# Attention outputs with channels on partitions, in a one-core layer of latent attention and gated linear attention

## The chip, the core and the metric

The kernel runs on one core of a Trainium2 chip. The metric is the device time of one execution in microseconds. Before the change it was 1341.73 us, the median of three runs (1340.36, 1341.73, 1341.91).

## The reference

One step of an encoder layer over 1024 prompt tokens and 64 tokens of a running stream, which has 512 cached frames. All is in float32. Cut to what the change touches:

```
mod = silu(c) @ w_ada + b_ada                      # six vectors per stream: shift, scale, gate, twice
h = rms_norm(x, g_norm1) * (1 + scale1) + shift1
c_q, c_kv, k_rope_raw, gq, gk, gv, g_lr, g_r = split(h @ w_in)

q = (rms_norm(c_q, g_q_lora) @ w_uq)               # 4 heads of 128 + 64
latent = concat([past_latent, rms_norm(c_kv, g_kv_lora)])
kv = latent @ w_ukv                                # per head 128 of key, 128 of value
k = concat([k_nope, krope])                        # the 64 rotary columns are the same for all heads
q, k = rms_norm(q, g_q_head), rms_norm(k, g_k_head)
q, k = rope on the last 64 columns
a_out = softmax(q k^T * scale, chunk-causal) @ v

b_out = rms_norm(gated linear attention) * silu(g_r)
x = x + gate1 * (concat([a_out, b_out]) @ w_out)
h2 = rms_norm(x, g_norm2) * (1 + scale2) + shift2
x = x + gate2 * (relu(h2 @ w_up)**2 @ w_down)
```

## The kernel before

Every large product is three products of a high and a low half (`mm3`, L92: high x high, low x high, high x low, in the type fp32r), so operands are split in two after they are made (`split`, L101, `split_T`, L954): ACT casts the high half, DVE subtracts it for the low half. Products of probabilities and values and all transposes are in plain float32. In the trace a plain product appears as two records on TensorE (PE), a transpose or an fp32r product as one.

The work of a stage is written as several generators, streams, that `interleave` (L47) advances by estimated times; the Tile framework's scheduler then puts the instructions of each engine in an order of its own, and each engine's queue runs in that order. DMAs are instructions of the queue that issues them, SP's nearly always; one that waits for its data holds all that stand behind it in that queue. Buffers come from pools with a fixed number of places: a load into a place waits until the last reader of its old content is done.

The stages in order of time:

- *Start* (to about 90 us). `start` (L399) loads x and the weights' first columns, `scale_rows` and `scale_end` make the modulation's scale for the first and then the second half of the channels. ACT takes squares of x (L337), multiplies x by the gain (`gained_x`, L380, high half on ACT, low half on DVE) and, with DVE, splits the first weights (`split_first`, L325). `shifts` makes the shift vector with `mod_vec` and loads the last tokens of x (`load_x(2)`).
- *Projections and gated linear attention* (to about 260 us). Its outputs go through PE transposes to channels on partitions and to the DRAM tile `mix_d`, channel blocks 4 to 7; the output gate goes to `r_d`.
- *Keys of the cached frames* (to about 360 us), `past_keys` (L1144), beside the last projections. A tile of 128 cached latents is loaded as it lies in memory, tokens on partitions. Two PE transposes (L1154) bring it to channels on partitions, ACT and DVE split it (`lath`, `latl`), and `keys_values` (L961) makes keys and values of four heads. There, after the norm, PE transposes the 128 plain columns of four heads (L1002), and the 64 rotary columns of four heads (`krt`, L1009), each head's twice side by side in 128 columns, so that the transposed tile holds them on partitions 0 to 63 and again on 64 to 127. ACT casts all (L1010), DVE takes the high half from the lower partitions (L1011): the high halves stand on partitions 0 to 63 and the low halves on 64 to 127 of `kv.kr`.
- *Attention* (to about 560 us). `keys_stream` and `queries_stream` make keys and queries of the prompt's tiles, three `worker` streams take units of one tile of queries and one head: the tile of the 64 sample tokens first (tile 8), then tiles 0 to 7. `attend` (L1069) makes the scores (L1080), their maximum, and the exponentials with their sum (L1091); DVE takes the sum's reciprocal. PE transposes the probabilities in blocks of 128 keys (L1117, evicted to `pt`, L1120), and the product with the values (L1107) has `pt` as its stationary operand and the values as the moving one: queries on partitions. ACT evicts it scaled by the reciprocal of the sum (L1132), which is one number per partition there, into `mo`. When four heads of a tile are done, `worker` transposes `mo` by four PE transposes (L1221), ACT copies them to `mt` (L1223) and writes `mt` from its own queue to `mix_d`, blocks 0 to 3 (L1224). Beside it, `mods` makes three further modulation vectors with `mod_vec`: row blocks of `w_ada` of 512 KB are loaded into three places `raw` (L166) and used by PE in order (L178). `wo_early` splits five blocks of the output weights.
- *Output projection* (to about 690 us). `out_early` (L1273) fetches `mix_d` and the gates for the first quarter of the tokens while attention's last tiles run, multiplies blocks 4 to 7 by the gate (`gate`, L1270) and splits all. `main` (L1423) does the same for the other three quarters (`mx`, `mr`, L1428), one quarter ahead of PE, then the products, the residual and the sums of squares.
- *The MLP*, with products of the Strassen kind, to the end. The change does not touch it.

Of the kernel before, what the change touches and what calls it, by code (L numbers as in the profile page):

```python
# [72 lines left out]
def layer(ctx: ExitStack, tc: tile.TileContext, I, O):  # L73
# [80 lines left out]
    c_d = dram.tile([16, P], F32, name="c_d")  # L154

# [80 lines left out]
    def has(*keys):  # L236
        return lambda: all(k in done or k in groups for k in keys)
# [59 lines left out]
    with ExitStack() as sctx:  # L297
# [92 lines left out]
        def start():  # L390
# [101 lines left out]
        def shifts():  # L492
# [5 lines left out]
            load_x(2)  # L498
            SP.dma_start(wg[0:16], I["w_gate_up"])
            SP.dma_start(wg[96:97], I["b_gate_up"])  # L500
            SP.dma_start(indi, I["gla_ind"])
            done.add("x 2")
            yield from vec
# [105 lines left out]
    with gctx:  # L609
# [7 lines left out]
        def load_past(t, place):  # L617

            past[t] = place
            SP.dma_start(past[t], I["cache_mla_latent"][t * P:(t + 1) * P])  # L620

        load_past(0, dp.tile([P, 256], F32, name="past", bufs=1))
# [338 lines left out]
    def keys_values(lh, ll, ki, tab, n, kv, slot, ahead=4500):  # L961
# [4 lines left out]
        R = kw.tile([P, 1, 2, 64], F32, name="R")  # L966
# [5 lines left out]
        DVE.tensor_tensor(out=R[:n, 0, :, 0:32], in0=a[:n, :, 0:32].broadcast_to([n, 2, 32]),  # L972
                          in1=t_[:n, :, 32:64].broadcast_to([n, 2, 32]), op=ALU.subtract)
        DVE.tensor_tensor(out=R[:n, 0, :, 32:64], in0=a[:n, :, 32:64].broadcast_to([n, 2, 32]),
                          in1=t_[:n, :, 0:32].broadcast_to([n, 2, 32]), op=ALU.add)
        kr = kw.tile([P, H, P], F32, name="krt", bufs=1)
        for g in range(2):
# [6 lines left out]
            for j in range(2):  # L984
                ACT.activation(kr[:n, 2 * g + j], pg[:, j, 0:P], AF.Square, accum_out=ss[:n, 2 * g + j:2 * g + j + 1])
# [9 lines left out]
        for g in range(2):  # L995
            DVE.tensor_tensor(out=kr[:n, 2 * g:2 * g + 2], in0=R[:n].rearrange("p t d c -> p t (d c)").broadcast_to([n, 2, P]),
                              in1=rs[g], op=ALU.mult)
# [10 lines left out]
        for hd in range(H):  # L1008
            PE.transpose(tp[:, hd, :n], kr[:n, hd], ident[:n, :n])  # L1009
        ACT.copy(kv.kr[:, :, cs], tp[:, :, :n])  # L1010
        DVE.tensor_tensor(out=kv.kr[64:P, :, cs], in0=tp[64:P, :, :n], in1=f32(kv.kr[64:P, :, cs]), op=ALU.subtract)  # L1011
# [57 lines left out]
    def attend(i, hd, n, off, kvs, nkeys, masked):  # L1069
# [25 lines left out]
        DVE.reciprocal(st[:n, 6:7], st[:n, 4:5])  # L1095
# [6 lines left out]
        def pv(args):  # L1102
            pt, k0, kn_ = args
            for k in range(kn_):
                kt = k0 + k
                kw = min(P, nkeys - P * kt)
                PE.matmul(op[:n, 0:P], lhsT=pt[:kw, k, :n], rhs=kvs[kt // 4].v[:kw, kt % 4, hd],  # L1107
# [22 lines left out]
        if i not in mos:  # L1130
            mos[i] = aw.tile([P, H, P], F32, name="mo")
        ACT.activation(mos[i][:n, hd], op[:n, 0:P], AF.Copy, scale=st[:n, 6:7])  # L1132
# [11 lines left out]
    def past_keys():  # L1144
        kvS.append(KV(kvA, 512))
        kvN.append(KV(kvA, 64))
        for t in (1, 2):
            load_past(t, kw.tile([P, 256], F32, name="latr"))
        for t in range(4):
            lt = past[t]  # L1150
            yield 600, 0, has("UK")
            tp = tp_bank()
            for b in range(2):
                PE.transpose(tp[:, b * P:(b + 1) * P], lt[:, b * P:(b + 1) * P], ident)  # L1154
            lh = kw.tile([P, 2, P], F32R, name="lath")
            ll = kw.tile([P, 2, P], F32R, name="latl")
            if t == 0:
                load_past(3, dp.tile([P, 256], F32, name="past", bufs=1))
            v = tp[:, 0:256].rearrange("p (b t) -> p b t", b=2)
            ACT.copy(lh, v)  # L1160
# [875 lines left out]
```

## Time and profile before

| what | value |
|---|---|
| median of the runs shown | 1341.73 us |
| the profiled execution's own time | 1340.44 us |
| its span, first to last instruction | 1338.3 us |
| granted TensorE clock | 1.00 |
| DVE, ACT busy | 68%, 49% |
| DMA traffic | 189.15 MB, 141 GB/s in the mean |

A row of a group reads: line, engine, operation, output <- inputs, partitions x elements, xcount, then busy time in us and mean ns of one instruction, and idle time of its engine ahead of it with what ended it. For matmuls the form `128*64 128x128` gives rows and columns of the stationary operand, then partitions and columns of the moving one. PE's records overlap, so a group's busy time is not the time that it keeps others away; for that one looks at the starts in a timeline. In a timeline a row has start and duration in us. Rows of stretches give each engine's busy us with the number of instructions, then the granted clock, the share of DMA and GB/s.

### The profile page before, as it was taken

Reading aid. Unit: us, or ns where it says so; the run is one execution under the profiler, and the core shown is the slowest. Engines: PE = TensorE matmul, PEld = TensorE weight load, DVE = VectorE, ACT = ScalarE, POOL = GpSimd, SP = SyncE. Lnnn points to the kernel's source line nnn. Section 1 sums busy time; section 2 is a strip of 40 time slices with the busy share of each in tenths; the row PEclk is TensorE's granted clock in tenths of the full one; section 3 lists DMA queues with packets and bytes.
Section 4 is the critical chain, followed back from the end, with each engine's and each line's share of the span. In section 5 each row is a group of like instructions: output and inputs, shape, how many; then the busy total and the mean of one; then the engine's idle time right before and its main releaser. Section 6 shows DMA issues by size and latency. Waiting matters only on the chain.

```text
span 1338.3 us, 25907 instructions
## 1 busy us (share of the span) xinstructions
PE 1316.3 (98%) x9986; PEld 1252.8 (94%) x9986; DVE 910.9 (68%) x2050; ACT 652.6 (49%) x1625; POOL 75.4 (6%) x136
## 2 busy tenths in 40 slices
PE   9999999999999999999999999999999999999999
PEld 8899999888767898999999999999999999999998
DVE  4898787466576756676899877565545965864553
ACT  5375554454266657543674444444444333343332
POOL 0100010132122200000000000000000000000000
PEclk9999999999999999999999999999999999999999
DMA  9420122374445200752537554443259755543440
GB/s 342 145 75 1 48 77 88 108 225 124 134 139 173 67 17 25 225 176 90 169 111 230 172 194 150 138 156 123 110 196 347 253 167 187 158 130 88 134 127 34
DMA packets 157957, 189.15 MB, mean 141 GB/s; under 512 B 14654, under 2 KB 109194, under 8 KB 157706
## 3 DMA queue, kind: packets, MB, share of 16 engines
q1 hardware_dynamic: 150554, 181.98, 42.6%
q10 hardware_dynamic: 7280, 5.52, 1.3%
q8 instruction: 78, 1.28, 0.4%
q14 instruction: 45, 0.37, 0.1%
HBM read 134.00 MB, written 53.47 MB: 140 GB/s over the span
## 4 chain that ended last, share of the span: by engine, by line
PE 77%; DVE 10%; ACT 4%; DMA 4%; issue 2%; POOL 2%; ACTq 0%; SPq 0%; DVEq 0%; POOLq 0%
PE mm L94 14%; PE mm L96 13%; PE mm L95 13%; PE g L94 5%; PE g L96 5%; PE g L95 5%; PE tp L94 3%; PE tp L96 3%; PE tp L95 3%; PE mm L1080 3%; PE g L1107 2%; PE g L882 1%; PE tp L1117 1%; DVE ts L1822 1%; DMA wg<-in_w_gate 1%
## 5 line engine op out<-in xcount | busy, mean ns | idle before, releaser
L102 ACT CAST opers<-quad 128x512 fp32r<-128x512 f32 x112 | 69.3, 620 | 185.1 <-PE mm L96 147.6
L103 DVE TENSOR_TENSOR opers<-quad,opers 128x512 fp32r<-128x512 f32 x112 | 77.1, 689 | 114.7 <-ACT opers L102 114.7
L94 PE MATMUL mm<-opers 128*128 128x272 f32 x448 | 128.5, 287 | 0.3 <-DVE e L1964 0.3
L96 PE MATMUL mm<-opers 128*128 128x272 f32 x448 | 128.7, 288 | 0.0
L95 PE MATMUL mm<-opers 128*128 128x272 f32 x448 | 128.2, 286 | 0.0
L94 PE MATMUL mm<-ah,wh 128*128 128x272 f32 x424 | 121.8, 288 | 0.0
L96 PE MATMUL mm<-ah,wl 128*128 128x272 f32 x424 | 121.8, 288 | 0.0
L95 PE MATMUL mm<-al,wh 128*128 128x272 f32 x424 | 121.7, 287 | 0.0
L94 PE MATMUL mm<-hh,wh 128*128 128x384 f32 (+2 forms) x264 | 91.1, 346 | 0.7 <-ACT wh L329 0.7
L95 PE MATMUL mm<-hl,wh 128*128 128x384 f32 (+2 forms) x264 | 87.2, 330 | 0.0
L96 PE MATMUL mm<-hh,wl 128*128 128x384 f32 (+2 forms) x264 | 86.6, 329 | 0.0
L94 PEld LDWEIGHTS mm<-opers 128*128 128x128 f32 x448 | 84.5, 189 | 0.5 <-issue 0.5
L96 PEld LDWEIGHTS mm<-opers 128*128 128x128 f32 x448 | 84.2, 188 | 0.0
L95 PEld LDWEIGHTS mm<-opers 128*128 128x128 f32 x448 | 84.0, 188 | 0.0
L94 PEld LDWEIGHTS mm<-ah,wh 128*128 128x128 f32 x424 | 79.9, 188 | 0.0
L95 PEld LDWEIGHTS mm<-al,wh 128*128 128x128 f32 x424 | 79.8, 188 | 0.0
L96 PEld LDWEIGHTS mm<-ah,wl 128*128 128x128 f32 x424 | 79.6, 188 | 0.1
L103 DVE TENSOR_TENSOR opers<-ru,opers 128x544 fp32r<-128x544 f32 x108 | 77.6, 719 | 2.3 <-ACT opers L102 2.0
L102 ACT CAST opers<-ru 128x544 fp32r<-128x544 f32 x108 | 69.4, 643 | 13.2 <-PE mm L96 10.9
L102 ACT CAST wh<-ru 128x512 fp32r<-128x512 f32 x67 | 41.1, 619 | 66.6 <-PE tp L95 21.0
L94 PE MATMUL mm<-wh,hh 128*128 128x264 f32 (+3 forms) x216 | 65.7, 304 | 0.0
L96 PE MATMUL g<-opers 128*128 128x272 f32 x224 | 64.7, 289 | 0.0
(416 smaller groups left out, 4247.2 us busy)
## 6 DMA issues: line engine op xcount, KB each, us to landing
ru<-u_d SPq DMA_DIRECT2D x108, 272.0 KB, 2.8
raw<-in_w_ada SPq DMA_DIRECT2D x32, 512.0 KB, 4.4
ru<-in_w_up SPq DMA_DIRECT2D x32, 512.0 KB, 4.1
quad<-in_w_down SPq DMA_DIRECT2D x16, 1024.0 KB, 6.5
u_d<-st SPq DMA_DIRECT2D x60, 272.0 KB, 2.1
u_d<-sc SPq DMA_DIRECT2D x45, 272.0 KB, 2.2
raw<-in_w_in SPq DMA_DIRECT2D x22, 256.0 KB, 3.5
x<-in_xo_T SPq DMA_DIRECT2D x8, 544.0 KB, 5.7
```

Source lines behind the costliest of these rows:

```text
L94: pin(PE.matmul(out, lhsT=ah, rhs=bh, start=first, stop=False, skip_group_check=more))
L95: pin(PE.matmul(out, lhsT=ah, rhs=bl, start=False, stop=False, skip_group_check=more))
L96: pin(PE.matmul(out, lhsT=al, rhs=bh, start=False, stop=last, skip_group_check=more))
L102: ACT.copy(hi, src)
L103: eng.tensor_tensor(out=lo, in0=src, in1=f32(hi), op=ALU.subtract)
L882: PE.matmul(sc[:n, a, p], lhsT=d[:, w * p + n * a:w * p + n * a + n], rhs=qv[:, :, p, a], start=True, stop=True)
L1080: PE.matmul(sp[:n, :w], lhsT=x[:, hd, :n], rhs=y[:, hd, :w], start=(j == 0), stop=(j == 4))
L1107: PE.matmul(op[:n, 0:P], lhsT=pt[:kw, k, :n], rhs=kvs[kt // 4].v[:kw, kt % 4, hd], start=(kt == 0), stop=(kt == nkt - 1))
L1117: PE.transpose(tp[:kw, k, :n], pr[k0 // 4][:n, P * k:P * k + kw], ident[:n, :n])
L1822: DVE.scalar_tensor_tensor(out=ts[s][:, 0:256], in0=w[:, ks], scalar=1.0, in1=cb[:, s, ks], op0=ALU.mult, op1=ALU.mult, accum_out=sums[:, ...
```

## The change

Four edits.

1. *Attention's output.* In `attend` the two operands of the product with the values change places: the values are the stationary operand and `pt` the moving one, so the product has channels on partitions and queries along its columns. ACT copies it to `mo` without a scale. The reciprocals of the sums go to a small tile `rsum`, tokens on partitions. When four heads are done, `worker` writes `rsum` to a new DRAM tile `rs_d` with heads as rows, four bytes a piece, and `mo` to `mix_d`, both from SP's queue. The four transposes, the copy `mt` and its write from ACT's queue are gone. `out_early` and `main` load the rows of `rs_d` spread over all partitions (`b0`, `b3`, `mb`) and multiply blocks 0 to 3 by them on DVE.
2. *Rotary keys.* The rotary columns of a key are no longer doubled. Two heads stand side by side in the 128 columns of one transpose, so two transposes take the place of four. ACT's cast and DVE's subtraction become two each, over 64 partitions and two heads: for the even heads the high halves stand on the lower partitions, for the odd heads on the upper ones, as it comes.
3. *Cached latents.* The kernel's input is the cached latents transposed. They are loaded with channels on partitions and split as they are.
4. *Start.* The squares of x's second half are taken ahead of the wait for the modulation, and the weights' split ahead of the gained x. `load_x(2)` is written in two parts.

```
@@ attend
-        DVE.reciprocal(st[:n, 6:7], st[:n, 4:5])
+        if i not in mos:
+            mos[i] = aw.tile([P, H, P], F32, name="mo"), aw.tile([P, H], F32, name="rsum")
+        mo, rsum = mos[i]
+        DVE.reciprocal(rsum[:n, hd:hd + 1], st[:n, 4:5])
...
-                PE.matmul(op[:n, 0:P], lhsT=pt[:kw, k, :n], rhs=kvs[kt // 4].v[:kw, kt % 4, hd],
+                PE.matmul(op[:, :n], lhsT=kvs[kt // 4].v[:kw, kt % 4, hd], rhs=pt[:kw, k, :n],
                           start=(kt == 0), stop=(kt == nkt - 1))
...
-        ACT.activation(mos[i][:n, hd], op[:n, 0:P], AF.Copy, scale=st[:n, 6:7])
+        ACT.copy(mo[:, hd, :n], op[:, :n])
@@ worker
-                yield 0, 700, None
-                tp = heads(tp_bank())
-                for hd in range(H):
-                    PE.transpose(tp[:, hd, :n], mos[i][:n, hd], ident[:n, :n])
-                mt = aw.tile([P, H, P], F32, name="mt", bufs=1)
-                ACT.copy(mt[:, :, :n], tp[:, :, :n])
-                ACT.dma_start(mix_d[:, 0:4, off:off + n], mt[:, :, :n])
-                yield 450, 0, None
+                mo, rsum = mos.pop(i)
+                SP.dma_start(rs_d[:, off:off + n].rearrange("h t -> t h"), rsum[:n])
+                SP.dma_start(mix_d[:, 0:4, off:off + n], mo[:, :, :n])
+                yield 0, 0, None
@@ out_early, main
+    def sums_row(k, kn, t0, n):
+        return rs_d[k:k + kn, t0:t0 + n].rearrange("(o h) t -> o h t", o=1).broadcast_to([P, kn, n])
...
-        t0, t1, r1 = fetch(mix_d, 0, 3), fetch(mix_d, 4, 2), fetch(r_d, 0, 2)
+        t0, b0, t1 = fetch(mix_d, 0, 3), fetch(rs_d, 0, 3), fetch(mix_d, 4, 2)
+        fetch(rs_d, 3, 1, b3)
         yield 0, 3000, None
+        gate(t0, b0)
         halves(0, 3, t0)
+        r1, t3 = fetch(r_d, 0, 2), fetch(mix_d, 3, 1)
...
+                    SP.dma_start(mx[3][:, :, o:o + n], sums_row(0, H, t0, n))
...
+                    gate(mx[0], mx[3])
                     split(mh[:, 0:4], ml[:, 0:4], mx[0], DVE)
@@ keys_values
-        for hd in range(H):
-            PE.transpose(tp[:, hd, :n], kr[:n, hd], ident[:n, :n])
-        ACT.copy(kv.kr[:, :, cs], tp[:, :, :n])
-        DVE.tensor_tensor(out=kv.kr[64:P, :, cs], in0=tp[64:P, :, :n], in1=f32(kv.kr[64:P, :, cs]), op=ALU.subtract)
+        for g in range(2):
+            PE.transpose(tp[:, g, :n], kr[:n, g], ident[:n, :n])
+        for e in range(2):
+            hi, lo = slice(64 * e, 64 * e + 64), slice(64 - 64 * e, P - 64 * e)
+            ACT.copy(kv.kr[hi, e::2, cs], tp[hi, 0:2, :n])
+            DVE.tensor_tensor(out=kv.kr[lo, e::2, cs], in0=tp[hi, 0:2, :n], in1=f32(kv.kr[hi, e::2, cs]), op=ALU.subtract)
@@ past_keys
-            tp = tp_bank()
-            for b in range(2):
-                PE.transpose(tp[:, b * P:(b + 1) * P], lt[:, b * P:(b + 1) * P], ident)
...
+            lh, ll = split_T(kw, past[t], 2, P, "lat")
@@ start
+            squares(0, sq, (4,))
             yield 0, 0, has("mod 1 1")
-            squares(0, sq, (4,))
             for k in range(4, KT):
-                gained_x(k, 0, pin)
                 if k % 2 == 0:
                     split_first(1, 0, (k // 2,))
+                gained_x(k, 0, pin)
@@ shifts
-            load_x(2)
...
-            yield from vec
+            load_x(2, (0,))
+            for n, step in enumerate(vec):
+                yield step
+                if n == 4:
+                    load_x(2, (4,))
...
```

More of the change, by code (lines that the diff above doesn't have):

```diff
@@ L154, in layer @@
     c_d = dram.tile([16, P], F32, name="c_d")
+    rs_d = dram.tile([H, TOK], F32, name="rs_d")
     def mod_rows(m, k):
@@ L619, in load_past @@
             past[t] = place
-            SP.dma_start(past[t], I["cache_mla_latent"][t * P:(t + 1) * P])
-        load_past(0, dp.tile([P, 256], F32, name="past", bufs=1))
+            SP.dma_start(place, I["past_T"][:, t * P:(t + 1) * P].rearrange("(b p) t -> p b t", p=P))
+        load_past(0, dp.tile([P, 2, P], F32, name="past", bufs=1))
         SP.dma_start(gkv_bc, I["g_kv_lora"].broadcast_to([P, 256]))
@@ L971, in keys_values @@
         DVE.tensor_tensor(out=t_[:n, 0], in0=kraw[:n, ki], in1=tabk[:n, tab, 1], op=ALU.mult)
[L972 to L976, printed above, removed]
+        DVE.tensor_tensor(out=R[:n, 0, 0:32], in0=a[:n, 0, 0:32], in1=t_[:n, 0, 32:64], op=ALU.subtract)
+        DVE.tensor_tensor(out=R[:n, 0, 32:64], in0=a[:n, 0, 32:64], in1=t_[:n, 0, 0:32], op=ALU.add)
+        kr = kw.tile([P, 2, P], F32, name="krt", bufs=1)
         for g in range(2):
@@ L994, in keys_values @@
             DVE.tensor_tensor(out=kn[:n, 2 * g:2 * g + 2], in0=kn[:n, 2 * g:2 * g + 2], in1=rs[g], op=ALU.mult)
-        for g in range(2):
-            DVE.tensor_tensor(out=kr[:n, 2 * g:2 * g + 2], in0=R[:n].rearrange("p t d c -> p t (d c)").broadcast_to([n, 2, P]),
-                              in1=rs[g], op=ALU.mult)
+        DVE.tensor_tensor(out=kr[:n].rearrange("p g (e c) -> p (g e) c", e=2), in0=R[:n].broadcast_to([n, H, 64]),
+                          in1=ss[:n, 4:8].rearrange("p (h o) -> p h o", o=1).broadcast_to([n, H, 64]), op=ALU.mult)
         cs = slice(P * slot, P * slot + n)
@@ L1147, in past_keys @@
         for t in (1, 2):
-            load_past(t, kw.tile([P, 256], F32, name="latr"))
+            load_past(t, kw.tile([P, 2, P], F32, name="latr"))
         for t in range(4):
-            lt = past[t]
             yield 600, 0, has("UK")
-            tp = tp_bank()
-            for b in range(2):
-                PE.transpose(tp[:, b * P:(b + 1) * P], lt[:, b * P:(b + 1) * P], ident)
-            lh = kw.tile([P, 2, P], F32R, name="lath")
-            ll = kw.tile([P, 2, P], F32R, name="latl")
-            if t == 0:
-                load_past(3, dp.tile([P, 256], F32, name="past", bufs=1))
-            v = tp[:, 0:256].rearrange("p (b t) -> p b t", b=2)
-            ACT.copy(lh, v)
-            DVE.tensor_tensor(out=ll, in0=v, in1=f32(lh), op=ALU.subtract)
-            yield 220, 1000, None
+            lh, ll = split_T(kw, past[t], 2, P, "lat")
+            if t == 0:
+                load_past(3, dp.tile([P, 2, P], F32, name="past", bufs=1))
+            yield 0, 1000, None
             yield from keys_values(lh, ll, 8 + t, t, P, kvS[0], t, 7000)
@@ L1276, in out_early, with fetch @@
         mh, ml = mix_pair()
+        b3 = mixh[0].tile([P, 1, HW], F32, name="b3")
         mixh.append((mh, ml))
-        def fetch(src, k, kn):
-            t = rawp.tile([P, kn, HW], F32, name="raw")
-            SP.dma_start(t, src[:, k:k + kn, 0:HW])
+        def fetch(src, k, kn, t=None):
+            t = rawp.tile([P, kn, HW], F32, name="raw") if t is None else t
+            SP.dma_start(t, sums_row(k, kn, 0, HW) if src is rs_d else src[:, k:k + kn, 0:HW])
             return t
@@ L1294, in out_early @@
         halves(6, 2, t2)
-        halves(3, 1, t3)
         yield 0, 2500, lambda: not units
```

21 lines of the change are left out of this document (12 added, 9 removed).

## The prediction

> **What bounds the kernel now.** I read the page's totals and the chain that ended last first, then the stretches that the change touches, then what PE waited for.
>
> ```profile
> span 1338.3 us, 25907 instructions
> PE 1316.3 (98%) x9986; PEld 1252.8 (94%) x9986; DVE 910.9 (68%) x2050; ACT 652.6 (49%) x1625; POOL 75.4 (6%) x136
> PE 77%; DVE 10%; ACT 4%; DMA 4%; issue 2%; POOL 2%; ACTq 0%; SPq 0%; DVEq 0%; POOLq 0%
> ```
>
> TensorE is busy in 98% of the span and holds 77% of the last chain. A busy PE need not be a full one, so the second look is at the stages: 260 to 360 us holds the keys of the cached frames beside the last projections, 360 to 560 attention, 560 to 690 the output projection. Behind them stand the largest of PE's waits there (us in total, times, longest).
>
> ```profile
> core 0: us, PE busy (x) PEld busy (x) DVE busy (x) ACT busy (x) POOL busy (x), PEclk, DMA share, GB/s
> 260.00:360.00 100.00, 95.77 (x601) 86.07 (x601) 55.51 (x146) 43.77 (x155) 20.57 (x40) 1.00 0.53 162
> 360.00:560.00 200.00, 193.81 (x1368) 161.47 (x1366) 139.47 (x415) 127.32 (x393) 28.34 (x46) 1.00 0.34 100
> 560.00:690.00 130.00, 129.81 (x1026) 128.78 (x1025) 100.21 (x215) 70.92 (x161) 4.99 (x8) 1.00 0.43 135
> ```
> ```profile
> PE tp L1117 <- ACT prob L1091: 2.6, 4, 1.1
> PE tp L1002 <- DVE kn L994: 2.1, 3, 0.9
> PE tp L1154 <- DVE kl L1004: 1.2, 3, 0.8
> ```
>
> PE stands idle for 4.2 us of the 100 and 6.2 us of the 200, at a granted clock of 1.00, and the longest of these waits is 1.1 us. So a matmul taken out of these stages should give back nearly the time that it holds PE. That is less than it lasts, since matmuls overlap; the timeline of PE shows it:
>
> ```profile
> 556.70 0.29 PE L96 MATMUL mm<-mh,wl 128*128 128x272 f32 x1
> 556.82 1.05 PE L1107 MATMUL g<-v,pt 128*128 128x128 f32 x8
> 557.63 0.37 PE L94 MATMUL mm<-mh,wh 128*128 128x272 f32 x1
> 557.84 0.29 PE L95 MATMUL mm<-ml,wh 128*128 128x272 f32 x1
> ...
> 558.10 0.60 PE L1221 MATMUL tp<-ident,mo 128*128 128x128 f32 x4
> 558.45 0.37 PE L94 MATMUL mm<-mh,wh 128*128 128x272 f32 x1
> ```
>
> Four transposes last 0.60 us, but the next matmul starts 0.35 us after the first of them, 0.088 us each. Eight records of probabilities times values hold PE for 0.81 us (556.82 to 557.63), 0.10 each. The first matmul behind a group takes 0.21 us to the next (557.63 to 557.84), where the pair ahead stands 0.12 apart: changing back costs some 0.09 us more, if the group goes as a whole.
>
> **The change part by part.** The groups that carry the terms: for TensorE least, median and longest ns of one; for the others busy us and mean ns.
>
> ```profile
> L1221 PE MATMUL tp<-ident,mo x36: 222/272/278, 412.0 to 558.4; 128*128 128x128 f32 x32, 64*128 64x64 f32 x4
> 411.97 0.46 PE L1221 MATMUL tp<-ident,mo 64*128 64x64 f32 x4
> L1009 PE MATMUL tp<-ident,krt x52: 222/272/329, 271.5 to 457.8; 128*128 128x128 f32 x48, 64*128 64x64 f32 x4
> L1154 PE MATMUL tp<-ident,past x4: 273/300/330, 260.4 to 304.1; 128*128 128x128 f32 x4
> L1107 PE MATMUL g<-v,pt 128*64 128x128 f32 x32 | 4.4, 279 | 0.0
> ```
> ```profile
> L996 DVE TENSOR_TENSOR krt<-R,ssk 128x256 f32<-128x256 f32 x24 | 9.9, 419 | 0.0
> L1010 ACT CAST kr<-tp 128x512 fp32r<-128x512 f32 x12 | 7.0, 585 | 3.7 <-PE tp L1009 3.4 <-issue 0.3
> L1132 ACT ACTIVATE mo<-g,sta 128x128 f32<-128x128 f32 x32 | 11.7, 368 | 9.4 <-PE g L1107 8.4 <-DVE sta L1087 0.6
> L1223 ACT COPY mt<-tp 128x512 f32<-128x512 f32 x8 | 4.7, 590 | 2.2 <-DMA mix_d<-mt 1.3 <-PE tp L1221 0.9
> L1271 DVE TENSOR_TENSOR mx<-mx,mr 128x1088 f32<-128x1088 f32 x3 | 3.9, 1287 | 1.6 <-DMA mx<-mix_d 1.6
> ```
>
> *Outputs of attention.* The product now comes out with channels on partitions, so the 36 transposes of L1221 go. Eight tiles at 0.35 us and the 64-token tile at some 0.25 are 3.1 us; with 0.09 each for changing back 3.9. I take 3.3, since several groups stand beside other transposes. ACT loses nine copies of 0.59 us (L1223), and its eviction of 0.37 us only drops the scale. PE's rows where the 64-token tile and the next one end, before:
>
> ```order
> L1117 MATMUL tp<-ident,prob 128x128
> L1221 MATMUL tp<-ident,mo 128x64 x4
> L178 MATMUL mm<-raw,scT 32x256 x4
> L1107 MATMUL g<-v,pt 128x128
> L1221 MATMUL tp<-ident,mo 128x128 x3
> L1054 MATMUL tp<-ident,qn 128x128 x4
> ```
>
> and now, with the lines renumbered (L1123 is the transpose of probabilities, L1113 the product, whose operands have changed sides):
>
> ```order
> L1123 MATMUL tp<-ident,prob 128x128
> L179 MATMUL mm<-raw,scT 32x256 x4
> L1113 MATMUL g<-pt,v 128x128
> L1057 MATMUL tp<-ident,qn 128x128 x4
> L1003 MATMUL tp<-ident,kn 128x128 x2
> ```
>
> Both groups of L1221 are gone, and the queries' transposes move up in their place.
>
> *Products of the 64-token tile.* For 128 tokens the swap changes no size. For the tile of 64 tokens 40 records (4 heads, 5 blocks of keys, two each) stream 64 columns in place of 128. The row of 64-column transposes gives (0.46 - 0.22) / 3 = 0.08 us a step against 0.10: 0.8 us; half the columns in half the time would be 2.0. I take 1.2, from 0 to 2.0. "TensorE: Matmul & The Clock Gate" of the Trainium skill (LDWEIGHTS) has the weight load follow the columns of the stationary operand, 107 ns for 128 of them; that operand grows here from 64 columns to 128, so by that rule this term is 0 and the sum below 1.2 us smaller. The 0.08 us in the row, whose stationary operand has 128 columns too, speaks against it.
>
> *Rotary keys.* Two heads share a transpose: 24 of 128 tokens and 2 of 64 go of L1009, at 0.088 to 0.11 us: 2.2 to 2.9, I take 2.6. DVE saves one product of 0.42 us a tile (L996); ACT's copy of 0.59 us (L1010) becomes two over half the partitions and half the width, and DVE's subtraction likewise. That lengthens the way to finished keys by at most 0.3 us a tile, under matmuls of other streams.
>
> *Cached latents.* They come transposed from memory, so eight transposes (four groups of two) and their evictions from PSUM go: 4 x (0.18 + 0.09) = 1.1 us, and with them the wait of 1.2 us for L1154 above. What is late next is the split of the latents, which no longer needs PE; I take 1.8 of 1.1 to 2.3.
>
> *Start.* The second square stands ahead of ACT's copy of the modulation now, and the weights' split ahead of the gained x.
>
> ```profile
> 24.21 0.27 ACT L475 COPY lat<-g 128x128 f32<-128x128 f32 x1 [4.90 <-PE g L470]
> 24.38 1.49 ACT L337 ACTIVATE sq<-hf 128x1536 f32<-128x1536 f32 x1
> 26.09 0.62 ACT L384 ACTIVATE hh<-hf,G 128x384 fp32r<-128x384 f32 x1 [0.23 <-DVE G L489]
> 27.27 0.45 PE L94 MATMUL mm<-hh,wh 128*128 128x384 f32 x1 [0.66 <-ACT wh L329]
> ```
>
> PE's wait of 0.66 us for the weights' split can go. But if the second half of x lands no earlier than 24.38, the copy waits 1.5 us for the square, and the modulation with it. Gain 0.4, from -1.0 to 0.7. The later change in loading x moves no row of SP's queue: nothing.
>
> *Division at the output projection.* DVE gets three more products like L1271 (1.29 us), and two smaller ones ahead of the early products in attention's last tiles. What is split last falls where DVE is nearly full:
>
> ```profile
> 660.00:680.00 20.00, 20.00 (x160) 19.77 (x159) 18.76 (x46) 18.43 (x52) 1.25 (x2) 1.00 0.04 13
> 700.00:720.00 20.00, 19.25 (x154) 19.03 (x153) 19.62 (x37) 10.03 (x21) 0.00 (x0) 1.00 0.66 227
> ```
>
> Their cover is that operands are made a quarter of the tokens ahead of PE. Without it five cost at most 5 x 1.29 = 6.4 us, three 3.9; I take 0.6.
>
> *Queues.* The writes of the outputs leave ACT's queue for SP's, each behind a write of sums in pieces of four bytes. SP's rows in attention, before (raw is the modulation's weights, cqr and latr are inputs of queries and keys):
>
> ```order
> L166 DMA raw<-in_w_ada 128x1024 x2
> L951 DMA latr<-lat_d 128x2x128
> L166 DMA raw<-in_w_ada 128x1024 x3
> L951 DMA cqr<-cq_d 128x3x128
> L166 DMA raw<-in_w_ada 128x1024 x7
> L951 DMA cqr<-cq_d 128x3x128
> ```
>
> and now:
>
> ```order
> L955 DMA latr<-lat_d 128x2x128
> L167 DMA raw<-in_w_ada 128x1024
> L1215 DMA rs_d<-rsum 64x4x1
> L167 DMA raw<-in_w_ada 128x1024
> L1216 DMA mix_d<-mo 128x4x64
> L167 DMA raw<-in_w_ada 128x1024
> L1215 DMA rs_d<-rsum 128x4x1
> L955 DMA cqr<-cq_d 128x3x128
> L167 DMA raw<-in_w_ada 128x1024 x2
> L1216 DMA mix_d<-mo 128x4x128
> ```
>
> The loads of three modulations, which ran through, now stand behind writes that wait for DVE's reciprocal and ACT's copy of the fourth head.
>
> ```profile
> raw<-in_w_ada SPq DMA_DIRECT2D x32, 512.0 KB, 4.4
> out_kr_p<-kraw SPq DMA_DIRECT2D x8, 32.0 KB, 1.8
> r_d<-r SPq DMA_DIRECT2D x4, 544.0 KB, 4.1
> L178 PE MATMUL mm<-raw,scT x152: 379/379/404, 364.7 to 431.8; 128*32 128x256 f32 x152
> ```
>
> PE takes a loaded row block every (431.8 - 364.7) / 19 = 3.5 us (eight records each), and three buffers make 10.6 us from one use of a buffer to its next. Less 4.4 us for the load, SP may stand for 6.2 us before PE waits. I expect shorter holds, price 0. The sums' own landing lies between 1.8 us (the smallest rows) and 4.1 (as many pieces, but long); they are read tens of us later. "DMA: Bandwidth & Descriptors" of the Trainium skill (Rules for kernel authors) says that a last dimension with strides becomes one descriptor per element, here 512 of four bytes; no run so far shows such a write.
>
> *Sum.* 3.3 + 1.2 + 2.6 + 1.8 + 0.4 - 0.6 = 8.7 us, in which the waits left in attention neither grow nor shrink; their order changes, so 3 us either way. The profiled execution took 1340.44 us, 2.1 more than its span: 1331.7 after. It is the second fastest of the runs shown, whose median of 1341.73 is 1.3 above it: forecast 1333.0.
>
> **The rivals.** *Attention is a chain, not a full PE.* If PE's order there is set by maximum, exponential and transposes, the work removed turns into waits for ACT (the 2.6 us of L1117 is the first such). The loss of 6.2 us in 200 speaks against it. Left are the parts outside, some 1.8 of the cached latents and 0.4, and half of the rest: 3 to 5 us, 1337.5.
>
> *SP's queue holds the loads.* The first three pairs of writes stand among the loads. A hold over 6.2 us reaches PE one for one; to use up 8.7 us the three must hold 6.2 + 2.9 = 9.1 us each. At 12 us they cost 17.4 and the time is 1350. For it: ACT and DVE deliver the fourth head at the end of a tile, and PE's uses come in bursts. Against it: the scheduler placed the loads between the writes, so that most buffers are free before.
>
> *Sums written slowly.* A write of 512 pieces could take far longer than the 4.1 us row; the program gives SP's transfers eight semaphores in turn, so an issue waits for the one eight before it, some 14 us here if every other is a load at 3.5. At 24 us a write would hold SP for 10, 3.8 beyond the slack, three times: +11.4, with the gain 1344. It shares the chance of the case before. The rule of the Trainium skill above ("DMA: Bandwidth & Descriptors", Rules for kernel authors) points this way.
>
> *Nothing to see.* The start goes wrong by 1.0, three of the division's products lie open at 3.9 and waits grow by 3: 8.7 - 1.4 - 3.3 - 3 = 1.0, 1340.7.
>
> **How the numbers follow.** A measurement here can tell about 0.2%, 2.7 us, from no change: faster means below 1339.0. Forecast (1328 to 1336.5) 0.76, chain 0.12, nothing to see 0.06, SP or sums 0.06. Forecast and chain are faster: 0.88; the others give 0.06 and 0.06. With every term at its good end, 3.9 + 2.0 + 2.9 + 2.3 + 0.7 + 3 = 14.8, it is 1327; the chain case ends at 1339. I give 1327 to 1339.
>
> **What would show it.** Right: L1221 and L1154 are gone, L1009's successor has 26 records, PE's idle time between 260 and 560 stays near 10 us, and the output projection begins some 8 us earlier. Wrong: PE waits for raw on L179, idle time in attention grown by what was removed, rs_d landing after more than 10 us, or PE waiting for DVE's products near 650 us.

## The result, and the profile after

The changed kernel takes 1365.25 us (median of 5 runs, 1361.36 to 1366.38), the kernel before 1340.36 in the same job: a ratio of 1.0170, 95% interval 1.0159 to 1.0181. The forecast was 1333.0, faster. It is 25 us slower. The profiled execution shown below is the slowest of the five.

The page of the kernel after, totals and last chain:

```profile
span 1364.3 us, 25803 instructions
PE 1319.9 (97%) x9916; PEld 1256.7 (92%) x9916; DVE 910.9 (67%) x2055; ACT 646.4 (47%) x1629; POOL 75.1 (6%) x136
PE 76%; DVE 9%; DMA 8%; ACT 4%; issue 2%; POOL 1%; SPq 1%; ACTq 0%; DVEq 0%; POOLq 0%
raw<-in_w_ada SPq DMA_DIRECT2D x32, 512.0 KB, 6.0
x<-in_xo_T SPq DMA_DIRECT2D x8, 544.0 KB, 6.4
```

DMA holds 8% of the chain where it held 4%, and the loads of the modulation's weights land after 6.0 us in the median where it was 4.4. The three stages (columns as in the prediction: busy time of PE, PEld, DVE, ACT and POOL, granted clock, DMA share, GB/s):

```profile
260.00:360.00 100.00, 96.25 (x606) 86.47 (x606) 57.79 (x157) 48.03 (x170) 21.68 (x42) 1.00 0.56 171
360.00:560.00 200.00, 184.75 (x1233) 152.78 (x1226) 131.87 (x402) 114.53 (x373) 26.90 (x44) 0.96 0.45 87
560.00:690.00 130.00, 115.95 (x879) 114.45 (x878) 80.81 (x167) 50.67 (x110) 3.71 (x6) 0.93 0.64 161
```

The stage of the cached frames is as good as before. In attention PE idles 15.3 us of 200 in place of 6.2, in the output projection 14.1 of 130 in place of 0.2, and the granted clock, 1.00 before, is 0.96 and 0.93. PE's largest waits:

```profile
PE g L96 <- DVE wol L106: 9.3, 1, 9.3
PE mm L179 <- DMA raw<-in_w_ada: 5.8, 3, 4.3
PE mm L1083 <- ACT prob L1094: 4.8, 3, 3.7
PE mm L94 <- ACT mh L102: 2.9, 1, 2.9
```

The two waits put down to DVE and ACT at the output projection end chains that begin with a transfer. The chain that ended last, in order of time, shows which (start, length, what):

```profile
398.05 16.78 DMA raw<-in_w_ada
...
535.75 11.16 DMA raw<-rs_d
...
561.90 22.89 DMA x<-in_xo_T
```

A load that lands after 4.4 us in the median of the kernel before took 16.8 here, and one of 5.7 us took 22.9. Each was issued while a write of sums was under way. The line between them is the read of the sums themselves, issued 3.5 us behind such a write. Those nine writes:

```profile
L1215 SPq DMA_DIRECT2D rs_d<-rsum x9: 360/367/615, 393.1 to 560.5; - x9
DMA to landing us min/median/max: 9.8/11.3/11.8
```

And what PE and the DMA engines do behind the last of them, issued at 560.5 (the columns are those of the stages above; the last three are granted clock, DMA share and GB/s):

```profile
566.00:570.00 4.00, 4.00 (x34) 4.00 (x33) 0.00 (x0) 0.00 (x0) 0.00 (x0) 1.00 0.69 32
570.00:574.00 4.00, 4.00 (x34) 4.00 (x33) 0.00 (x0) 0.00 (x0) 0.00 (x0) 1.00 0.91 31
574.00:578.00 4.00, 3.73 (x30) 3.51 (x28) 0.00 (x0) 0.00 (x0) 0.00 (x0) 1.00 1.00 28
578.00:582.00 4.00, 0.00 (x0) 0.00 (x0) 0.00 (x0) 0.00 (x0) 0.00 (x0) 0.88 0.53 76
582.00:584.00 2.00, 0.00 (x0) 0.00 (x0) 0.00 (x0) 0.00 (x0) 0.00 (x0) 0.50 1.04 320
586.00:588.00 2.00, 1.00 (x4) 1.00 (x5) 2.00 (x3) 1.21 (x2) 0.00 (x0) 0.50 0.40 132
```

The DMA engines are busy and move 28 to 32 GB/s for 12 us, a tenth of the 320 that they move once the write has gone through. The trace's packets say the same: the four-byte ones take 9 ns each and nearly all have started by 566, but packets of 512 bytes, 28 ns each at 562, take 97 to 1224 ns on average in the slices from 564 to 578, and 27 again at 582. DVE and ACT stand still, PE runs out at 578, and comes back at half its clock.

Where the 26 us between the spans went: PE idles 1364.3 - 1319.9 = 44.4 us where it idled 1338.3 - 1316.3 = 22.0, which is 22.4 more. Its busy time is 3.6 more although work was removed. The run noload below has no such holes and nine small transposes more, and shows 1308.2 at a clock of 1.00. Less some 0.8 for these nine I estimate that the kernel's own matmuls need 1307.4; the other 12.5 of PE's busy time are the lowered clock. 22.4 + 12.5 - 8.9 = 26.0 then follows, where 8.9 is the work removed (1316.3 - 1307.4). The trace's record of the clock has four stretches of 0.50 between 413.8 and 608.3 us, 34.1 us in all. At half speed they could cost up to 17.1 us; PE stands idle in part of them.

### The profile page after: what moved, and what is told of

It reads as the page before. It is cut to its first block, busy times and chain, and to the rows that moved or that the text cites. A ratio compares the mean times of both kernels' runs of the same rounds, so it can differ in the third digit from the quotient of the medians.

```text
span 1364.3 us, 25803 instructions
## 1 busy us (share of the span) xinstructions
PE 1319.9 (97%) x9916; PEld 1256.7 (92%) x9916; DVE 910.9 (67%) x2055; ACT 646.4 (47%) x1629; POOL 75.1 (6%) x136
## 4 chain that ended last, share of the span: by engine, by line
PE 76%; DVE 9%; DMA 8%; ACT 4%; issue 2%; POOL 1%; SPq 1%; ACTq 0%; DVEq 0%; POOLq 0%
PE mm L94 13%; PE mm L96 13%; PE mm L95 13%; PE g L94 5%; PE g L96 5%; PE g L95 5%; PE tp L94 3%; PE tp L96 3%; PE tp L95 3%; PE mm L1083 2%; DMA raw<-in_w_ada 2%; DMA x<-in_xo_T 2%; PE g L886 2%; PE g L1113 2%; PE mm L179 1%
## 5 line engine op out<-in xcount | busy, mean ns | idle before, releaser
L94 PE MATMUL mm<-opers 128*128 128x272 f32 x448 | 128.4, 287 | 0.3 <-DVE e L1968 0.3
L94 PE MATMUL mm<-ah,wh 128*128 128x272 f32 x424 | 121.8, 288 | 0.0
L94 PE MATMUL mm<-hh,wh 128*128 128x384 f32 (+2 forms) x264 | 90.7, 344 | 0.2 <-ACT hh L385 0.2
L94 PEld LDWEIGHTS mm<-opers 128*128 128x128 f32 x448 | 84.5, 189 | 0.5 <-issue 0.5
L94 PEld LDWEIGHTS mm<-ah,wh 128*128 128x128 f32 x424 | 79.9, 188 | 0.0
L94 PE MATMUL mm<-wh,hh 128*128 128x264 f32 (+3 forms) x216 | 65.5, 303 | 0.0
```

Source lines behind the costliest of these rows:

```text
L94: pin(PE.matmul(out, lhsT=ah, rhs=bh, start=first, stop=False, skip_group_check=more))
```

## The experiments

**The theory and its rivals.** *Pieces*: the four-byte writes choke the DMA engines, and the rest gains what was forecast. *Holds*: loads stand on SP's queue behind writes that wait for DVE and ACT. *Order*: attention's new order and the added products cost the time. Every ratio is to the kernel before, run in turn in the same job.

**rows**

```diff
+tp = tp_bank()
+PE.transpose(tp[:H, :n], rsum[:n], ident[:n, :n])
+rt = aw.tile([H, P], F32, name="rt4")
+DVE.tensor_copy(rt[:, :n], tp[:H, :n])
-SP.dma_start(rs_d[:, off:off + n].rearrange("h t -> t h"), rsum[:n])
+SP.dma_start(rs_d[:, off:off + n], rt[:, :n])
```

> The changed kernel with one edit: the sums of a tile (128 tokens x 4 heads) are turned by one PE transpose into four rows and written as rows of 512 bytes, in place of 512 pieces of four bytes. Three theories. Pieces: writes in four-byte pieces choke the DMA engines for some 10 us each, and what is issued behind them comes late; without them the rest of the change gives its 8.7 us less about 1 for nine transposes and copies: 1330 to 1338. Holds: the loads stand on SP's queue behind writes that wait for DVE and ACT; these waits are all still there: above 1350. Order: attention's new order and the added products cost the time: above 1355.

Measured: 1338.34 us, ratio 0.9983 (0.9974 to 0.9991). One edit takes 25 us away (1.0170 less 0.9983 is 0.0187 of 1340). Attention's order and the added products are still there, so order falls. SP still stands 67.1 us in total before the writes of the outputs, for ACT's copies, so holds falls:

```profile
SPq L1220 <- ACT mo L1136: 67.1, 7, 20.3
```

But 2 us of gain are not 7.7.

**actq**

```diff
-SP.dma_start(rs_d[:, off:off + n].rearrange("h t -> t h"), rsum[:n])
+ACT.dma_start(rs_d[:, off:off + n].rearrange("h t -> t h"), rsum[:n])
```

> The changed kernel with one edit: the writes of the sums in four-byte pieces are issued on ACT's queue, those of the outputs stay on SP's. Pieces, as a matter of the DMA engines that both queues use: transfers issued within 10 us behind such a write still take 10 us and more, 1352 to 1370. Pieces, as a matter of one queue's order alone: SP's loads run past them, 1330 to 1340. Holds: half of the waiting writes have left SP, about 1345.

Measured: 1356.16 us, ratio 1.0117 (1.0103 to 1.0130). The write is as slow on the other queue, and most of the loss stays:

```profile
rs_d<-rsum ACTq DMA_DIRECT2D x8, 2.0 KB, 11.2
```

"DMA: Bandwidth & Descriptors" of the Trainium skill (Issuing engines are not separate DMA queues) says that transfers of either queue run on the same 16 engines; the 11.2 us agree. The kernel gains some 7 us by the move (1.0170 against 1.0117); the runs don't show which wait gave them.

**dummy4, dummy16, dummysp, dummysp4**: the kernel before, with the reciprocals in a tile of their own that is also written to memory and read by nobody. In the traces PE, ACT, DVE and POOL run the same instructions in the same order as before; the four runs differ only in the layout of the write.

```diff
+SP.dma_start(rs_d[:, off:off + n].rearrange("h t -> t h"), rsum[:n])        # dummy4:   4 B, 4 B apart
+SP.dma_start(rs_d[off:off + n], rsum[:n])                                   # dummy16:  16 B, 16 B apart
+SP.dma_start(rs_d[:, off:off + n, 0].rearrange("h t -> t h"), rsum[:n])     # dummysp:  4 B, 64 B apart
+SP.dma_start(rs_d[:, off:off + n, 0].rearrange("h t -> t h"), rsum[:n])     # dummysp4: 4 B, 16 B apart
```

> The kernel before with one thing added: the reciprocal sums of each tile, gathered in one small tile, are also written to memory in four-byte pieces on SP's queue, and nobody reads them. No instruction of PE, ACT or POOL moves; SP's queue gets nine writes. Pieces: 1350 to 1368, with raw, x or the weights of the output projection landing more than 10 us after their issue. Holds: the writes wait for DVE only, and each for a short time: 1341 to 1350. Order: 1340 to 1342, nothing of PE's order changes.

> As the run before it (the kernel before with nine writes of sums that nobody reads, at the same places of SP's queue), but laid out by token, so that a write is 128 pieces of 16 bytes in place of 512 of four. Pieces, if their number sets the time: a quarter of the hold, 2 to 3 us, mostly hidden: 1340 to 1346. Pieces, if it is bytes per line of memory: about as the run before, 1350 and more. Holds: the same as the run before, since the writes wait for the same instructions.

> The kernel before with nine writes of sums that nobody reads, 512 pieces of four bytes each as in the run that cost 30 us, but each piece 64 bytes from the next in memory. If neighbouring pieces hold each other up, since several of the 16 engines write into one line of memory at once: 1340 to 1346. If the number of pieces sets the time: 1365 to 1372 again.

> The kernel before with nine writes of sums that nobody reads, 512 pieces of four bytes each, 16 bytes from one to the next (4 bytes apart cost 30 us, with 10.3 us to landing; 64 bytes apart cost nothing, with 2.6 us). If only pieces that lie in one line of 64 bytes hold each other up, a quarter as many do: landing after 4 to 5 us, 1341 to 1348. If the line is 16 bytes or less: 1340, as at 64. If the line is longer than 64 bytes or it is the number of writes per page: 1365.

Measured: dummy4 1370.54 us, ratio 1.0219 (1.0203 to 1.0234); dummy16 1340.96, 1.0004 (0.9995 to 1.0013); dummysp 1340.35, 1.0000 (0.9991 to 1.0009); dummysp4 1342.97, 1.0024 (1.0013 to 1.0035). The time from issue to landing of the nine writes, in dummy4, dummy16, dummysp and dummysp4:

```profile
DMA to landing us min/median/max: 7.5/9.6/15.7
```
```profile
DMA to landing us min/median/max: 1.4/2.3/6.3
```
```profile
DMA to landing us min/median/max: 2.0/2.8/6.3
```
```profile
DMA to landing us min/median/max: 2.9/3.2/6.2
```

The suspected write alone, put into the kernel before, costs 30 us: the cause is shown from both sides. The loads of the output weights show how, in dummy4 (first line) and dummysp:

```profile
raw<-in_w_out SPq DMA_DIRECT2D x8, 512.0 KB, 11.7
raw<-in_w_out SPq DMA_DIRECT2D x8, 512.0 KB, 5.2
```

My own picture of it was wrong in one point. It is not the number of pieces alone: 512 pieces of four bytes cost nothing if they lie 64 bytes apart, 3 us at 16 and 30 us at 4. Pieces of four bytes side by side hold each other up, and with them whatever the DMA engines have in flight. Sharing 64 bytes of memory is not enough: in dummy16 and in dummysp4 four pieces lie in 64 bytes, and the writes land after 2.3 and 3.2 us (I had expected 4 to 5 for dummysp4). So the hold arises between pieces closer than 16 bytes. Why is open; that different DMA engines write into one short stretch of memory at the same moment is a guess, since the traces don't tell the engines apart.

**Where the rest of the gain is: noload, nogate, earlymb.** In the run with rows PE waits once for 2.1 us near 588, for the second norm's statistics, and the clock falls to 0.53 behind it:

```profile
PE tp L1510 <- DVE dg L1506: 2.1, 1, 2.1
```
```profile
585.00:588.00 3.00, 0.89 (x7) 0.63 (x5) 2.25 (x8) 0.60 (x2) 1.20 (x2) 1.00 0.87 234
588.00:592.00 4.00, 3.94 (x17) 3.53 (x16) 3.44 (x11) 2.18 (x6) 0.00 (x0) 0.53 1.03 333
```

The profiled execution of rows is the slowest of its eleven; four of the eleven have a mean granted clock of 1.000 and take 1335.09 to 1338.34 us. The DMA engines are full near 588, and the change loads the sums over 128 partitions just ahead of it, 544 KB for each of three quarters of the tokens.

```diff
 # noload, on rows
-SP.dma_start(mx[3][:, :, o:o + n], sums_row(0, H, t0, n))
-gate(mx[0], mx[3])
+gate(mx[0], mx[2])
 # nogate, on rows
-gate(mx[0], mx[3])
 # earlymb, on rows: b2 is loaded in out_early and stands for mx[3] where c == 2
+SP.dma_start(b2[:, :, o:o + n], sums_row(0, H, t0, n))
```

> The run with the sums written as rows, less the four loads of sums for the output projection (544 KB each, spread over 128 partitions); the products stay, by the gates' tile instead, so the outputs of attention are multiplied by the wrong factors. It asks where the rest went: written as rows, the change gives 2 us where 7.7 were worked out, and PE waits 2.4 us near 585 and then runs at a lowered clock. Loads: these transfers fill the DMA engines while the inputs of the second operand are loaded, it comes late, and what stands behind its products on DVE with it: 1332 to 1335. Products: DVE's three added ones at 1.29 us are what holds the statistics of the second norm up: 1337 to 1339. Neither, the loss lies in attention: 1338.

> The run with the sums written as rows, less the three late products with the sums on DVE; the loads stay and nobody reads them, so the outputs of attention of three quarters of the tokens are not divided. Loads: 1337 to 1339. Products: 1332 to 1335. Neither: 1338. Both in one chain (late inputs, then a longer row of products): both runs fall to 1332 to 1335.

> The run with the sums written as rows, with one edit: the sums for the second operand of the output projection are loaded into a tile of their own beside the early products, some 30 us sooner. If the loads that crowd the DMA engines ahead of that operand are the 2.8 us: 1335.5 to 1336.5, and no wait of 2 us near 585. If the products on DVE hold the second norm up by themselves: 1338, and the wait stays.

Measured: noload 1335.50 us, ratio 0.9967 (0.9954 to 0.9980); nogate 1337.76, 0.9985 (0.9975 to 0.9995); earlymb 1338.35, 0.9986 (0.9977 to 0.9996). Leaving the loads out gives 2.8 us by the medians and 2.1 by the ratios (0.9983 against 0.9967), whose intervals touch. Leaving the products out gives 0.6 by the medians and nothing by the ratios: within the scatter. Moving the first of the loads gave nothing. PE's wait for the statistics was 1.1 us in noload (first line) and 2.8 in earlymb:

```profile
PE tp L1508 <- DVE dg L1504: 1.1, 1, 1.1
PE tp L1515 <- DVE dg L1511: 2.8, 1, 2.8
```

What DVE waited for ahead of these statistics, in rows (first line) and in earlymb:

```profile
579.84 1.29 DVE L1267 TENSOR_TENSOR mx<-mx,mb 128x1088 f32<-128x1088 f32 x1 [2.85 <-DMA mx<-mix_d]
585.29 1.16 DVE L1482 SCALAR_TENSOR_TENSOR x<-mm,modT,x 128x208 f32<-128x208 f32 x4 [2.19 <-DMA x<-in_xo_T]
```

In rows it is the outputs for the third operand of the projection, whose load is issued at 573.64 us (in noload at 568.50). In earlymb that load is early, and the load of x behind it is late. The statistics start at 586.36 us in both, at 583.68 in noload. So no single transfer is in the way; that the sums' loads together make the DMA engines late there is the likely reading, not a separate test.

The profiled execution of noload, the fastest of its runs, is the one in which the forecast's work can be read without holes:

```profile
PE 1308.2 (98%) x9925; PEld 1246.9 (94%) x9925; DVE 913.7 (69%) x2064; ACT 646.6 (49%) x1629; POOL 75.2 (6%) x136
```

**The parts by themselves: krt, lat, three, nokrt.** krt is the kernel before with the changed `keys_values`; lat has the cached latents and the start; three has both; nokrt is rows with `keys_values` as before.

```diff
 # krt and three have these lines, nokrt has those of before
-for hd in range(H):
-    PE.transpose(tp[:, hd, :n], kr[:n, hd], ident[:n, :n])
+for g in range(2):
+    PE.transpose(tp[:, g, :n], kr[:n, g], ident[:n, :n])
```

> The kernel before with the rotary keys' part of the change alone: two heads share a transpose, 52 become 26. By the term of the forecast 2.6 us less (2.2 to 2.9): 1337.4 to 1338.1 where the kernel before takes 1340.3. If attention is a chain in which removed work turns into waits: half of it, 1339.

> The kernel before with the cached latents' part and the start's part of the change alone: the cached latents come transposed from memory, the second squares stand ahead of the modulation's copy, the split of weights ahead of the gained x. By the terms of the forecast 1.8 + 0.4 us less (0.1 to 3.0): 1338.1 where the kernel before takes 1340.3. If the latents' wait is only moved: 1339.5 to 1340.5.

> The kernel before with the rotary keys', the cached latents' and the start's parts of the change, without the product's new form, its sums and its divisions. By the forecast's terms 2.6 + 1.8 + 0.4 = 4.8 us less: 1335.5. By what the parts did alone (+3.4 and -1.8): 1342. If the product's new form is worth its 4.5 less 1 for the transposed rows, this run stands 3.5 us above the run with rows and without loads (1335.5): 1339.

> The run with the sums written as rows, with the rotary keys made as in the kernel before (52 transposes). Alone that part made the kernel 3.4 us slower where 2.6 less were forecast. If it costs as much in company: 1335 where the run with rows takes 1338.3. If PE's freed time counts there and the loss alone was an accident of the order that it left: 1341. If it is worth nothing in attention, a chain: 1338.

Measured: krt 1343.85 us, ratio 1.0033 (1.0017 to 1.0048); lat 1338.61, 0.9990 (0.9980 to 0.9999); three 1341.77, 1.0011 (0.9998 to 1.0024); nokrt 1341.31, 1.0004 (0.9995 to 1.0013). By these medians the rotary keys' part has no price of its own. It costs 3.4 us alone (4.4 by the ratio), and some 0.0021 or 2.8 us on top of lat; with the new product it gains the same 0.0021 (rows 0.9983 against nokrt 1.0004). In krt PE's work does fall by 2.5 us (1316.3 to 1313.8), and its idle time grows by 5.3:

```profile
PE 1313.8 (98%) x9960; PEld 1249.2 (93%) x9960; DVE 908.5 (68%) x2050; ACT 654.2 (49%) x1638; POOL 75.5 (6%) x136
```
```profile
PE tp L1116 <- ACT prob L1090: 3.5, 4, 1.8
PE tp L999 <- DVE kn L992: 3.2, 4, 1.0
PE tp L1501 <- DVE dg L1497: 1.8, 1, 1.8
```

The wait for the exponential stood at 2.6 us, that for the scaled keys at 2.1; the third was 0.2.

The clock is part of the loss on top of lat. Nine of three's twelve runs have a mean granted clock of 0.995 or 0.996 and take 1341.0 to 1345.5 us. The three at 1.000 take 1335.80, 1335.83 and 1338.62, where the forecast's terms gave 1335.5 and the ten runs of lat at 1.000 have a median of 1338.4. The profiled execution of three is one of the nine. Its clock falls in attention and stays down for 10.2 us:

```profile
392.35:395.76 3.41, 2.51 (x16) 1.67 (x17) 2.10 (x9) 2.49 (x9) 0.00 (x0) 1.00 0.38 141
395.76:399.17 3.41, 3.41 (x19) 2.16 (x20) 0.81 (x4) 1.11 (x4) 0.00 (x0) 0.50 0.21 62
```

So as far as three runs can tell, the part gains some 2 us on top of lat too while the clock holds. krt's seven runs at 1.000 have a median of 1342.55, so alone it costs some 2 us even then.

Where each trace stands against the kernel before, by the start of the same matmul (us, profiled executions; the columns are the first product of the queries' projection, the last transpose of probabilities, the 65th L94 matmul of the output projection, and the end of the span; before at 356.5, 554.3, 594.2, 1338.3):

| kernel | queries | attention ends | projection | end |
|---|---|---|---|---|
| after | -5.7 | +6.3 | +25.2 | +25.9 |
| dummy4 | +0.3 | +17.4 | +29.2 | +30.9 |
| dummysp | -1.2 | -0.9 | -1.1 | -0.2 |
| rows | -5.4 | -6.9 | -1.9 | -0.1 |
| noload | -6.1 | -7.7 | -6.7 | -6.8 |
| lat | -5.0 | -4.0 | -3.3 | -2.3 |
| krt | -1.1 | -0.1 | +1.5 | +2.8 |

dummysp differs from before by nothing but writes that cost nothing, so 1 us in a cell means little. The profiled execution of after and that of rows are the slowest of their runs, that of noload the fastest, so the last column sets rows and noload too far apart: 6.7 us, where the medians give 2.8. The median lead of lat's matmuls grows from 1.4 us at 255 us to 5.0 at 320, while dummysp's stays at 1.2 to 1.3. So the cached latents are worth some 3.6 us where they are computed, twice what was forecast, and half of it is given back later. The start's part can't be told: at 90 us lat leads by 0.8 and dummysp, whose start is unchanged, by 0.7.

**A better place for the division: tilediv, tilediv_nokrt, tilediv3, divstream, divstream3.** All write rows, read them back over 128 partitions tile by tile, multiply on POOL, and then write the outputs; the output projection is that of before.

```diff
 # tilediv: in the attention worker, behind the write of the rows; tilediv_nokrt: with before's keys
+yield 0, 4000, None
+mb = aw.tile([P, H, P], F32, name="mb")
+SP.dma_start(mb[:, :, :n], sums_row(0, H, off, n))
+yield 0, 4000, None
+POOL.tensor_tensor(out=mo[:, :, :n], in0=mo[:, :, :n], in1=mb[:, :, :n], op=ALU.mult)
 # tilediv3 and divstream3: bufs=3 for mo and rsum
 # divstream and divstream3: the same steps in a stream of their own
-interleave([..., worker(), worker(), worker(), out_early()])
+interleave([..., worker(), worker(), worker(), divider(), out_early()])
```

> The run with the sums written as rows, but the division is made in attention: each tile's rows are read back over 128 partitions as soon as they are written, POOL multiplies the outputs by them, and then they are written; the output projection loads no sums and multiplies by none, as in the kernel before. The forecast's 8.7 less some 1 for nine transposes, with the 2.8 of the loads and the 0.6 of the products that the runs so far showed gone: 1333 to 1336. If SP's queue stands behind the two more waits for each tile: 1340 and more, with PE waiting for raw.

> As the run before it, with the rotary keys made as in the kernel before. If the rotary keys' part costs 3.4 in any company: 1330 to 1333. If it gives its 2.6: 1336 to 1339. The pair of this run and the one before it, and the pair with and without it in the runs with rows, must agree for either to be believed.

> The run that divides in attention, with three buffers in place of two for a tile's outputs and sums. If the late exponentials came from ACT standing before a buffer of outputs that the division still held: the 10 us of waits for the exponential fall to about 3, and the time to 1333 to 1337. If they came from SP's queue or from POOL's products: 1348 to 1352 again.

> The division in attention (rows written, read back over 128 partitions, POOL multiplies, outputs written), but as a stream of its own beside the three attention workers, with two buffers for a tile's outputs. If the 10 us of late exponentials came from a worker that stood still in the order: 1333 to 1337, and PE's wait for the exponential back at about 3 us. If they came from SP's queue or POOL: 1348 to 1352 again.

> As the run before it, with three buffers for a tile's outputs and sums. If the buffers are held too long with the division in attention: 2 to 5 us less than the run before it. If they are not: the same within 1 us.

Measured: tilediv 1350.11 us, ratio 1.0071 (1.0058 to 1.0084); tilediv_nokrt 1352.61, 1.0088 (1.0075 to 1.0101); tilediv3 1350.19, 1.0076 (1.0062 to 1.0089); divstream 1336.85, 0.9981 (0.9972 to 0.9990); divstream3 1337.69, 0.9980 (0.9971 to 0.9989). The first two miss their main forecasts by some 14 us. tilediv's other branch, 1340 and more with PE waiting for raw, fits by the time, but PE waits 2.8 us for raw and 10.2 for the exponential; tilediv3 lies in the range given for SP's queue or POOL. The wait for the exponential in tilediv (first) and in divstream:

```profile
PE tp L1123 <- ACT prob L1094: 10.2, 5, 3.0
```
```profile
PE tp L1123 <- ACT prob L1094: 2.5, 3, 1.3
```

My first reason, buffers held too long, fell with tilediv3. SP's queue and POOL fell with divstream, which has the same transfers and products. The second reason fits: one of three workers stood still in the written order while the division's two transfers were allowed for (4 us each), so that its next unit came late. It is not shown alone, since divstream also allows 3 us in place of 4 and orders all of attention anew. divstream beats the kernel before by 3.2 us (2.5 by the ratio) and the changed kernel by some 25 (1.0170 against 0.9981), but not the run with rows by more than the scatter. The pair tilediv and tilediv_nokrt puts the gain of the rotary keys at 0.0017 or 2.3 us, with intervals that overlap; rows and nokrt gave 2.8.

## Why the prediction was wrong, point by point

- **The queues: this step failed.** "The sums' own landing lies between 1.8 us (the smallest rows) and 4.1 (as many pieces, but long); they are read tens of us later", price 0. The landing measured 11.3, and the price 25 us (1.0170 against 0.9983 with rows). Two things were wrong. The upper bound was taken from a write of 512 pieces of 1088 bytes each; there was no row for neighbours of four bytes, and I treated the row as a bound. And I asked only who reads the sums and how long SP may stand. Who pays is whoever has a transfer in flight beside the pieces, on either queue. "Read tens of us later" was wrong too: the first read was issued 12.4 us after the last write that it needs, and SP stood 11.3 us for that write to land. That is not the price, since dummy4, whose sums nobody reads, loses as much.
- **The rival "sums written slowly" named the right write and the wrong way.** It let a write cost something only from 14 us on, when SP's eight semaphores come round, and gave 1344 with 0.06 for two cases. At 11.3 us SP would have stood for nothing by that reckoning. The rule of the Trainium skill that I quoted beside it ("DMA: Bandwidth & Descriptors", Rules for kernel authors: one descriptor per element) holds as to the number (510 packets of four bytes start between 562 and 564 us), and dummysp shows that the number is not the price. It spoke against the change, and I set it aside since no run showed such a write; with a bound that reached it, the range would have had to reach the 1365 measured.
- **The signs named ahead.** Those for right came for the work: L1221 and L1154 are gone and L1009's successor has 26 records. The other two for right did not come: PE's idle time between 260 and 560 us is 19.0 us where some 10 were named, and the output projection is late, not early. Three of those for wrong came: the sums landed after more than 10 us, PE waited for raw on L179, and the idle time in attention grew by 9.1 us.
- **PE's work: right.** Forecast 3.3 + 1.2 + 2.6 and 1.1 of the latents' transposes, 8.2; noload's PE is busy 8.1 us less, with some 0.8 for nine transposes of sums that the forecast did not have. The 3 us allowed for attention's waits held in noload (7.0 us of idle time in 360 to 560 us against 6.2), not in the changed kernel.
- **The product's new form: its gain in time stays open.** 3.3 + 1.2 - 0.6 less about 1 for the rows is 2.9; rows against three is 0.0028 of 1340, 3.8 us. That looks right, but three's low clock may be what makes the difference: its three runs at 1.000 (1335.80, 1335.83, 1338.62) are no slower than the four of rows (1335.09 to 1338.34). The 64-column step and its rule were not tried apart.
- **Rotary keys: 2.6 is right beside the new product (2.8, and 2.3 in the other pair), wrong alone (+3.4).** That "the waits left in attention neither grow nor shrink" failed there: PE's idle time in krt grows by 5.3 us over the whole span, of which 1.0, 1.2 and 1.7 lie in the three stages from 260 to 690 us.
- **Cached latents and start: 2.2 forecast, 1.8 measured** by the medians and 1.3 by the ratio, within 0.1 to 3.0. There is luck in that: some 3.6 us are gained at the cached latents and half is given back.
- **Division: its loads were left out.** The text priced five products on DVE and no transfer; noload puts 2.1 to 2.8 us on the loads. The products' 0.6 is too small to tell.
- **The lowered clock was not in any term.** By the estimate above it is 12.5 of the 26 us.

## What to carry to other kernels

Price a transfer by what it does to the transfers behind it, not only by who waits for its own data; a 2 KB write cost 30 us over nine uses because of how its pieces lie in memory. Where the trace has no row of the same kind, size, spacing and direction, the nearest row is not a bound. A kernel with PE at 98% can pay twice for a hole of 2 us or more, once for the hole and once for the clock behind it. Freed work in one stage is worth what the written order lets through to the end: measure parts together as well as alone, and look at the granted clock of every run before a small difference is put down to a part.

## What the runs showed of the hardware

Pieces of four bytes, 512 to a write (medians): 4 bytes apart 9.6 to 11.3 us to landing, 16 apart 3.2, 64 apart 2.8, while 128 pieces of 16 bytes side by side take 2.3. During the slow one at 560.5 us the DMA engines read as 0.69 to 1.00 busy and move 28 to 32 GB/s, a tenth of the 320 behind it.

The granted clock stayed at 1.00 through waits of up to 1.1 us in the kernel before. Behind a wait of 2.1 us in rows it was 0.50 for 6.8 us, and in the changed kernel it fell during a wait of 4.3 us and was 0.50 for 6.8:

```profile
412.00:414.00 2.00, 0.00 (x0) 0.00 (x0) 0.00 (x0) 0.00 (x0) 0.00 (x0) 0.94 0.48 104
414.00:416.00 2.00, 1.03 (x9) 0.25 (x9) 0.00 (x0) 0.00 (x0) 0.00 (x0) 0.50 0.75 168
416.00:418.00 2.00, 2.00 (x14) 2.00 (x10) 0.01 (x1) 0.58 (x1) 0.00 (x0) 0.50 1.00 277
418.00:420.00 2.00, 2.00 (x9) 1.77 (x9) 1.36 (x5) 0.46 (x2) 0.00 (x0) 0.50 0.58 221
```

"TensorE: Matmul & The Clock Gate" of the Trainium skill (Part 1: The HAM clock gate) gives half the clock after an idle window of about 3.4 us that runs free of the kernel; the half agrees, and a drop behind 2.1 us of waiting, with PE busy for 0.9 of the 3 us around it, shows that a shorter wait can be enough.

The length of one wait does not decide it. Waits of 1.8 us in krt and one of 2.3 us in tilediv (at 559.0) left the clock at 1.00, behind 1.9 us in dummysp4 it fell, and in three it fell with no wait over 0.9 us in the 3.4 us ahead, in which PE was busy for 2.51. In the traces' records of the clock every stretch at 0.50 ahead of a kernel's last 3 us lasts 3.4, 6.8 or 10.2 us.
